# First passes of the down projection from the eleventh pair on, residual kept in DRAM meanwhile

## The chip, the cores and the metric
The kernel runs on one core of a Trainium2 chip. The metric is the device time of one execution in microseconds (us); lower is better. Engines in the profile: PE (matmuls) and PEld (weight loads into it), DVE (vector), ACT (activation), POOL, and SP, which here issues nearly all transfers (DMA). Each engine works through its instructions in a fixed order.

## The reference
One layer of an encoder on 256 tokens of width 2048, in float32: a mixer (latent attention and a two-way state-space scan, gated and added), then a gated MLP with a short convolution, then a final norm. The change lies in the MLP:

```
h = h + m @ W_out
h = h + conv_ffn(rms_norm(h, norm_ffn_w), ...)
out = rms_norm(h, norm_final_w)

def conv_ffn(h, w_up, conv_w, conv_b, w_down):
    u = centred_dwconv(h @ w_up, conv_w, conv_b)      # kernel of 3 over the tokens
    gate, val = jnp.split(u, 2, axis=-1)              # 5632 columns each
    return (jax.nn.silu(gate) * val) @ w_down         # 5632 -> 2048
```

## The kernel before
Channels lie on the 128 partitions, tokens run along a row. A float32 product is made of three products of rounded parts: each operand is split into a high part (made by ACT, line 220 or 150) and a low part (the difference, made by DVE, line 221 or 151). Weights are loaded from DRAM in slabs of 128 columns and 16 blocks of 128 rows (1 MB), into three buffers (`raw`), and split in halves of 8 blocks (`wh`, `wl`) into five pairs of buffers. L247 is the product of the high weights with both parts of the activations, L254 that of the low weights.

The MLP's first half, the up projection, has 44 pairs of slabs, a gate slab and a value slab each, numbered m = 0 to 43. The two slabs of a pair run as mates: both high products (32 matmuls of L247), then both low ones (32 of L254). The result goes through the convolution (L296, L297, L1093, L1095), the gate and a split to `aHL`, on ACT and DVE; two pairs make one tile of `aHL` (4 KB per partition) and one of sums, `aS`.

The norm before the up projection is done in two ways. For m under 9 (`TURNED`) the activations `hHL` are not scaled yet, and `conv3` multiplies by `r_ffn` (L1092). Meanwhile `rescale(j)`, j = 0 to 7, makes the scaled blocks (`nF`, L1082, L1083, L151) from the residual `h`, one in each of the pairs 1 to 8; from pair 9 on they are used.

The down projection's first 8 of 16 output blocks use a scheme of seven products on 2 x 2 blocks. Its first pass for two pairs of slabs, one tile kp of 22, is a unit (`unit_one`, 12 matmuls of L1142): it needs one weight load of 1 MB, sums of weights on DVE (L185, L186, L188, L189, tiles `T13`, `T24`) and their split (L150, L151). Units are put between pairs of the up projection, by the table `first` (pair m to kp). After a unit, part of `aS` goes to DRAM (`n4D`), and for kp under K0 also `aHL` (`aD`), so that its place is free.

After the up projection come the plain output blocks 8 to 15 (`down`: `d8`, ... for the second part of the rows, `a8`/`b8`, ... for the first part, L1243 adds into `h`), mixed with the second passes (`second`: `s20`, ...) and at the end the first 8 blocks (`seven_channels`, L1218). The list `seq` gives the order; `a_load` (L1208) and `n4_load` (L1204) bring back what was stored.

Tiles of 4 KB per partition come from one pool of 29 (`page`). The residual is in four of them, `hp[0]` to `hp[3]`, from the output projection to the end. A scheduler of the framework sets the order on each engine from the order in which the code emits, the dependences and its own estimates.

Of the kernel before, what the change touches and what calls it, by code (L numbers as in the profile page):

```python
# [8 lines left out]
F32 = mybir.dt.float32  # L9
# [6 lines left out]
P = 128  # L16
S = 256
# [47 lines left out]
def tile_bidir_hybrid_layer(ctx: ExitStack, tc, xT, pos, vec, cst, w_in, w_r, w_v, w_qk, w_oa,  # L65
                            w_os, w_out, w_up, w_dn, out, RAWB=3, HB=5, NPG=29, NP1=18):
    nc = tc.nc
# [5 lines left out]
    dr = ctx.enter_context(tc.tile_pool(name="dr", bufs=1, space=bass.MemoryType.DRAM))  # L73
# [3 lines left out]
    def page(shape, dt=F32, name="pg"):  # L77
        return pp.tile(shape, dt, tag="pg", bufs=NPG, name=name)
# [10 lines left out]
    def f32(ap):  # L89
        return ap.bitcast(F32)  # L90
# [17 lines left out]
    def vcol(name, i=0):  # L108
        o = VOFF[name] + i
        return V[:, o:o + 1]  # L110
# [38 lines left out]
    def hilo(wh, wl, v):  # L149
        act.activation(wh, v, AF.Copy)  # L150
        dve.tensor_sub(wl, v, f32(wh))  # L151
# [887 lines left out]
    hp, hHL = {}, {}  # L1039
# [37 lines left out]
    def rescale(j):  # L1077
        v = page([P, 2, S], name="nF")
        t = nF[j] = page([P, 2, 2, S], F32R, name="hHL")
        for b in range(2):  # L1080
            m = 2 * j + b
            act.activation(v[:, b, :], hp[m // 4][:, m % 4, :], AF.Identity, scale=vcol("nffn", m))  # L1082
        dve.tensor_mul(v, v, r_ffn["r"].unsqueeze(1).broadcast_to([P, 2, S]))  # L1083
        hilo(t[:, 0], t[:, 1], v)

    gv, aHL = {}, {}

# [212 lines left out]
    def at(slot, fn, *a):  # L1300
        late.append((slot, lambda: fn(*a)))
# [156 lines left out]
        at(b + max(4 * q, 0), x_load, q)  # L1458
    b = len(jobs)
    turns = [b]  # L1460
    K0, KE = 12, 14
    first = {7 + (36 * kp + 10) // 20: kp for kp in range(21)}
    assert len(first) == 21 and all(2 * kp + 2 <= m < NFF for m, kp in first.items())
    slots = []
    for m in range(NFF):
# [5 lines left out]
    for j in range(8):  # L1471
        at(slots[1 + j] + j % 2, rescale, j)
# [3 lines left out]
    lo, rest_of = {}, {}  # L1476
# [16 lines left out]
    turns.append(lo["d8"])  # L1493
    for g, w in enumerate("s20 b10 b11 d8 d10 s16".split()):
        at(lo[w], n4_load, g, min(4, NK - 4 * g))
    for kp in range(K0):
        at(lo["u21"] + (4 * kp) // 5 if kp < 10 else lo["a8"] + kp - 10, a_load, kp)
    for i in range(4):
        at(lo["a13"] + 1 + i, seven_channels, i)
    jobs[b].post.append(ffn_r)  # L1500
# [86 lines left out]
    while i < len(jobs):  # L1587
        j = jobs[i]
        first = base[i]
# [109 lines left out]
```

## Time and profile before
| | us |
|---|---|
| three runs | 1934.26, 1937.96, 1938.18; median 1937.96 |
| profiled execution | 1937.51 |
| its span (first to last instruction) | 1935.7 |
| output projection, last part, and up projection | about 1106 to 1762 of the span |
| down projection | about 1751 to 1925 |

A time of the profile is counted from the span's start. An engine's row gives start, length, engine, line, the tile written and those read, and how many such instructions are merged; a bracket gives the idle time before it and what ended it. DVE rows of before and after differ in line numbers by 8 (L1095 is L1103 after).

### The profile page before, as it was taken

To read this page: it belongs to the slowest core of one execution; us is meant where nothing else is said; L and a number is where in the kernel's file an instruction comes from. 1 tells how busy PE (TensorE), PEld (TensorE's weight loads), DVE (VectorE), ACT (ScalarE), POOL (GpSimd) and SP (SyncE) were. 2 spreads that over 40 slices of the span, in tenths; PEclk is the share of its full clock that TensorE was granted. 3 is DMA by queue.
4 is the path that set the end of the run, shared out by engine and by line. 5 is a ranking of instruction groups with operands and counts; after the bars stand their busy time and mean duration, and the time that the engine had idled before them with its cause. 6 is when DMAs were issued, how large, how long until landed. Compare 5 with 4: busy or idle time off the path is not lost.

```text
span 1935.7 us, 28865 instructions
## 1 busy us (share of the span) xinstructions
PE 1919.9 (99%) x10800; PEld 1677.9 (87%) x10800; DVE 1616.4 (84%) x2645; ACT 1286.4 (66%) x2049; POOL 16.2 (1%) x36
## 2 busy tenths in 40 slices
PE   9999999999999999999999999999999999999997
PEld 8899988888888888888888888888888888888887
DVE  7888778979779779779898886889889888888676
ACT  6565555878887888878665555765666666565554
POOL 0200000000000000000000000000000000000000
PEclk9999999999999999999999999999999999999999
DMA  7644547765665665565566675657666666668994
GB/s 284 206 156 150 164 132 228 273 220 174 215 230 168 212 239 169 202 239 169 173 195 201 216 250 176 214 199 245 243 235 233 223 223 217 212 238 306 315 292 143
DMA packets 171291, 415.20 MB, mean 214 GB/s; under 512 B 10640, under 2 KB 113744, under 8 KB 144272
## 3 DMA queue, kind: packets, MB, share of 16 engines
q1 hardware_dynamic: 169360, 410.74, 62.5%
q0 software_dynamic: 1024, 1.54, 0.3%
q8 instruction: 84, 1.38, 0.3%
q10 hardware_dynamic: 768, 1.09, 0.2%
q14 instruction: 55, 0.45, 0.1%
HBM read 398.56 MB, written 13.60 MB: 213 GB/s over the span
## 4 chain that ended last, share of the span: by engine, by line
PE 93%; DVE 3%; DMA 2%; ACT 1%; issue 0%; SPq 0%; DVEq 0%; ACTq 0%
PE g L247 37%; PE g L254 19%; PE g L965 11%; PE s L1142 5%; PE g L282 3%; PE g L283 3%; PE g L284 3%; PE s L965 2%; DMA raw<-in_w_dn 1%; PE g L226 1%; PE g L228 1%; PE g L227 1%; DVE wl L221 1%; PE s L247 1%; PE s L870 1%; PE s L879 1%
## 5 line engine op out<-in xcount | busy, mean ns | idle before, releaser
L221 DVE TENSOR_TENSOR wl<-raw,wh 128x1024 fp32r<-128x1024 f32 x590 | 708.6, 1214 | 173.9 <-ACT wh L220 95.3
L220 ACT ACTIVATE wh<-raw 128x1024 fp32r<-128x1024 f32 x590 | 609.4, 1048 | 254.3 <-PE g L247 82.2
L247 PE MATMUL g<-xHL,wh 128*128 128x512 f32 x1424 | 341.7, 392 | 0.2 <-DVE cu L297 0.2
L247 PE MATMUL g<-hHL,wh 128*128 128x512 f32 x1408 | 328.2, 390 | 0.0
L247 PEld LDWEIGHTS g<-hHL,wh 128*128 128x128 f32 x1408 | 263.4, 188 | 53.8
L247 PEld LDWEIGHTS g<-xHL,wh 128*128 128x128 f32 x1424 | 262.5, 188 | 52.1 <-PE s L228 0.4
L254 PEld LDWEIGHTS g<-xHL,wl 128*128 128x128 f32 x1424 | 182.6, 191 | 6.9
L254 PE MATMUL g<-xHL,wl 128*128 128x256 f32 x1424 | 184.7, 283 | 0.0
L254 PEld LDWEIGHTS g<-hHL,wl 128*128 128x128 f32 x1408 | 174.8, 192 | 3.4
L254 PE MATMUL g<-hHL,wl 128*128 128x256 f32 x1408 | 176.0, 283 | 0.0
L965 PE MATMUL g<-wh,yHL 128*128 128x512 f32 x392 | 124.9, 390 | 0.0
L150 ACT ACTIVATE wh<-raw 128x1024 fp32r<-128x1024 f32 (+1 forms) x108 | 80.5, 776 | 52.0 <-PE g L965 13.1
L151 DVE TENSOR_TENSOR wl<-raw,wh 128x1024 fp32r<-128x1024 f32 (+1 forms) x108 | 91.0, 876 | 23.1 <-ACT wh L150 15.1
L150 ACT ACTIVATE wh<-T 128x1024 fp32r<-128x1024 f32 x60 | 63.6, 1061 | 56.8 <-DVE T L189 21.4
L282 PE MATMUL g<-wh,xHL 128*128 128x512 f32 x256 | 100.4, 392 | 0.0
L283 PE MATMUL g<-wl,xHL 128*128 128x512 f32 x256 | 100.0, 391 | 0.0
L284 PE MATMUL g<-wh,xHL 128*128 128x512 f32 x256 | 99.8, 390 | 0.0
L1095 DVE SCALAR_TENSOR_TENSOR uc<-u,V,uc 128x255 f32<-128x255 f32 x176 | 84.6, 481 | 15.9 <-ACT uc L1093 14.8
L965 PEld LDWEIGHTS g<-wh,yHL 128*128 128x128 f32 x392 | 73.6, 188 | 15.2
L151 DVE TENSOR_TENSOR wl<-T,wh 128x1024 fp32r<-128x1024 f32 x60 | 73.4, 1223 | 15.8 <-ACT wh L150 13.2
L247 PE MATMUL g<-aHL,wh 128*128 128x512 f32 x338 | 79.8, 390 | 0.2 <-ACT wh L220 0.2
L1093 ACT ACTIVATE uc<-u,V 128x256 f32<-128x256 f32 x88 | 52.4, 595 | 40.9 <-DVE u L297 34.3
(389 smaller groups left out, 3120.0 us busy)
## 6 DMA issues: line engine op xcount, KB each, us to landing
raw<-in_w_in SPq DMA_DIRECT2D x88, 1024.0 KB, 4.9
raw<-in_w_up SPq DMA_DIRECT2D x88, 1024.0 KB, 4.8
raw<-in_w_in SPq DMA_DIRECT2D x128, 256.0 KB, 3.9
raw<-in_w_os SPq DMA_DIRECT2D x32, 1024.0 KB, 6.2
raw<-in_w_dn SPq DMA_DIRECT2D x30, 1024.0 KB, 5.1
raw<-in_w_oa SPq DMA_DIRECT2D x16, 1024.0 KB, 5.8
FB<-acsD SPq DMA_DIRECT2D x32, 512.0 KB, 7.3
raw<-in_w_dn SPq DMA_DIRECT2D x16, 896.0 KB, 5.1
```

The lines of the kernel that those rows point to most:

```text
L150: act.activation(wh, v, AF.Copy)
L151: dve.tensor_sub(wl, v, f32(wh))
L220: act.activation(vh, r, AF.Copy)
L221: dve.tensor_sub(vl, r, f32(vh))
L247: pe.matmul(ps, lhsT=wh[:, b, :], rhs=x, start=k == 0, stop=False)
L254: pe.matmul(cell["ps"][:, 0, :], lhsT=wl[:, b, :], rhs=get(k)[:, 0, :], start=False, stop=k == ktot - 1)
L282: pe.matmul(ps, lhsT=x[:, 0, ts], rhs=wH[:, kk, :], start=k == 0, stop=False)
L283: pe.matmul(ps, lhsT=x[:, 0, ts], rhs=wL[:, kk, :], start=False, stop=False)
L284: pe.matmul(ps, lhsT=x[:, 1, ts], rhs=wH[:, kk, :], start=False, stop=k == kt - 1)
L965: pe.matmul(M[nm], lhsT=x, rhs=w, start=left[nm] == total[nm], stop=left[nm] == 1)
L1095: dve.scalar_tensor_tensor(o[:, a], u[:, b], vcol("fcw", k * 88 + cb), o[:, a], ALU.mult, ALU.add)
L1142: pe.matmul(M[nm], lhsT=x, rhs=w, start=left[nm] == 3 * NK, stop=left[nm] == 1)
```

## The change
- `first`: the first unit comes after pair 10 instead of pair 7, and the 21 units of the up projection lie 33/20 pairs apart instead of 36/20. After pairs 10, 12, 13, 15, 17, 18, 20, ... 43 instead of 7, 9, 11, 12, 14, 16, ... 43.
- Each block of the residual is written to DRAM (`hD`) once two rescalings have read it, and its page is given up; four reads (`h_load`) bring it back: blocks 2 and 3 at `d8` and `d10`, blocks 0 and 1 at `a12` and `b12`.
- K0 is 10 instead of 12: ten tiles of `aHL` go to DRAM and back instead of twelve.

```
     def rescale(j):
...
+        if j % 2:
+            nc.sync.dma_start(hD[j // 2], hp.pop(j // 2))
+
+    hD = dr.tile([4, P, 4, S], F32, name="hD")
+
+    def h_load(q):
+        hp[q] = page([P, 4, S], name="h")
+        nc.sync.dma_start(hp[q], hD[q])
...
-    K0, KE = 12, 14
-    first = {7 + (36 * kp + 10) // 20: kp for kp in range(21)}
+    K0, KE = 10, 14
+    first = {10 + (33 * kp + 10) // 20: kp for kp in range(21)}
...
+    for q, w in ((2, "d8"), (3, "d10"), (0, "a12"), (1, "b12")):
+        at(lo[w], h_load, q)
     for kp in range(K0):
-        at(lo["u21"] + (4 * kp) // 5 if kp < 10 else lo["a8"] + kp - 10, a_load, kp)
+        at(lo["u21"] + (4 * kp) // 5 if kp < 8 else lo["a8"] + kp - 8, a_load, kp)
```

DVE's order behind the last weight half of pair 7 (`wl<-raw_12663` before, `wl<-raw_12666` after). `raw_12708` before is the first unit's weights; `raw_12712` and `raw_12788` after are the slabs of pair 8. Before:

```order
L221 TENSOR_TENSOR wl_12685<-raw_12663,wh_12684 128x1024
L151 TENSOR_TENSOR hHL_12666<-nF_12665,hHL_12666 128x512
L297 TENSOR_TENSOR u_12696<-u_12696,g_12617 128x256
L1092 TENSOR_TENSOR u_12696<-u_12696,r_ffn_11954 128x256
L1095 SCALAR_TENSOR_TENSOR uc_12697<-u_12696,V_72,uc_12697 128x255 x2
L1108 TENSOR_TENSOR uc_12697<-uc_12697,uc_12655 128x256
L1113 TENSOR_TENSOR aHL_12705<-uc_12697,aHL_12705 128x256
L1083 TENSOR_TENSOR nF_12710<-nF_12710,r_ffn_11954 128x512
L297 TENSOR_TENSOR u_12781<-u_12781,g_12727 128x256
L185 TENSOR_TENSOR T13_12719<-raw_12708 128x512
L151 TENSOR_TENSOR hHL_12711<-nF_12710,hHL_12711 128x512
L186 TENSOR_TENSOR T13_12719<-raw_12708 128x512
```

After, the same place:

```order
L221 TENSOR_TENSOR wl_12689<-raw_12666,wh_12688 128x1024
L151 TENSOR_TENSOR hHL_12669<-nF_12668,hHL_12669 128x512
L297 TENSOR_TENSOR u_12700<-u_12700,g_12620 128x256
L221 TENSOR_TENSOR wl_12722<-raw_12712,wh_12721 128x1024
L1100 TENSOR_TENSOR u_12700<-u_12700,r_ffn_11955 128x256
L1103 SCALAR_TENSOR_TENSOR uc_12701<-u_12700,V_72,uc_12701 128x255 x2
L221 TENSOR_TENSOR wl_12768<-raw_12712,wh_12767 128x1024
L1116 TENSOR_TENSOR uc_12701<-uc_12701,uc_12658 128x256
L297 TENSOR_TENSOR u_12779<-u_12779,g_12725 128x256
L221 TENSOR_TENSOR wl_12791<-raw_12788,wh_12790 128x1024
L1121 TENSOR_TENSOR aHL_12709<-uc_12701,aHL_12709 128x256
L1083 TENSOR_TENSOR nF_12714<-nF_12714,r_ffn_11955 128x512
```

The unit's sums (L185, L186) are gone from here, and the weight halves of pair 8 stand in between; the rescaling (L1083, L151) keeps its place among the convolution's rows.

DVE's order at the last first-pass unit, `u21`, between `d8`/`d9` and `d10` (`h_11272` and `h_17397` are block 2 of the residual, `g` the sums of `d8` and `d9`). Before:

```order
L189 TENSOR_TENSOR T24_17397<-T24_17397,raw_17390 128x512
L151 TENSOR_TENSOR wl_17395<-T13_17396,wh_17394 128x1024
L151 TENSOR_TENSOR wl_17447<-T24_17397,wh_17446 128x1024
L1243 TENSOR_TENSOR h_11272<-h_11272,g_17404 128x256
L221 TENSOR_TENSOR wl_17463<-raw_17460,wh_17462 128x1024
L1243 TENSOR_TENSOR h_11272<-h_11272,g_17404 128x256
```

After:

```order
L189 TENSOR_TENSOR T24_17402<-T24_17402,raw_17393 128x512
L151 TENSOR_TENSOR wl_17400<-T13_17401,wh_17399 128x1024
L1251 TENSOR_TENSOR h_17397<-h_17397,g_17409 128x256
L151 TENSOR_TENSOR wl_17452<-T24_17402,wh_17451 128x1024
L1251 TENSOR_TENSOR h_17397<-h_17397,g_17409 128x256
L221 TENSOR_TENSOR wl_17468<-raw_17465,wh_17467 128x1024
```

The first add into `h`, which now needs a read from DRAM, stands between the unit's two low halves. SP's order of transfers at the same place, before:

```order
L144 DMA raw_17488<-in_w_dn 128x2048
L1204 DMA n4_17392<-n4D_89 128x4x256
L1208 DMA aHL_17490<-aD_88 128x1024
L1208 DMA aHL_17492<-aD_88 128x1024
L1157 DMA n4D_89<-aS_17363 128x128 x2
```

and after:

```order
L144 DMA raw_17493<-in_w_dn 128x2048
L1212 DMA n4_17395<-n4D_90 128x4x256
L1092 DMA h_17397<-hD_88 128x1024
L1216 DMA aHL_17495<-aD_89 128x1024
L1216 DMA aHL_17497<-aD_89 128x1024
```

The read of block 2 takes the first reload's place, and the reloads of `aHL` come one place later.

## The prediction
> **What bounds the kernel now.** I read the page's head first, then busy time by stretches, then the PE's own rows where a stretch was short of work. The head:
> ```profile
> span 1935.7 us, 28865 instructions
> PE 1919.9 (99%) x10800; PEld 1677.9 (87%) x10800; DVE 1616.4 (84%) x2645; ACT 1286.4 (66%) x2049; POOL 16.2 (1%) x36
> ```
> PE is busy for 1919.9 of 1935.7 us, and the change takes no matmul away. What it can win is time in which PE waits or runs slow. The stretches (us, busy time of PE, PEld, DVE, ACT, POOL, clock, DMA share, GB/s) show where:
> ```profile
> 1153.00:1175.00 22.00, 22.00 (x128) 19.41 (x127) 15.12 (x25) 11.30 (x16) 0.00 (x0) 1.00 0.56 199
> 1242.00:1264.00 22.00, 22.00 (x128) 19.46 (x127) 20.59 (x38) 15.77 (x29) 0.00 (x0) 1.00 0.65 221
> 1344.00:1358.00 14.00, 14.00 (x78) 12.24 (x77) 12.85 (x23) 7.71 (x14) 0.00 (x0) 1.00 0.72 242
> 1787.00:1803.00 16.00, 16.00 (x88) 13.93 (x87) 10.64 (x17) 5.92 (x8) 0.00 (x0) 1.00 0.83 268
> 1838.00:1860.00 22.00, 21.76 (x110) 18.28 (x109) 16.61 (x20) 14.56 (x20) 0.00 (x0) 1.00 0.99 303
> ```
> (Pairs of slabs are numbered from 0, as in the code.) In these stretches PE is never idle, but for 0.24 us in the last. DVE is busy for 20.59 of 22 us in pairs 4 and 5, where rescaling is on, and for 12.85 of 14 in a pair that a down unit follows. So DVE is a close second, and at the end DMA is one, with 0.99 of the time. The one large gap is at the first down unit (start, length, group; in brackets the idle time before and what ended it):
> ```profile
> 1276.22 7.44 PE L247 MATMUL g<-hHL,wh 128*128 128x512 f32 x32
> 1283.50 3.99 PE L254 MATMUL g<-hHL,wl 128*128 128x256 f32 x32
> 1289.84 0.73 PE L1142 MATMUL s<-wh,aS 128*128 128x512 f32 x2 [2.35 <-ACT wh L150]
> 1291.42 0.79 PE L1142 MATMUL s<-wl,aS 128*128 128x512 f32 x1 [0.86 <-DVE wl L151]
> 1303.89 4.00 PE L254 MATMUL g<-hHL,wl 128*128 128x256 f32 x32
> ...
> 1339.95 4.00 PE L254 MATMUL g<-hHL,wl 128*128 128x256 f32 x32
> 1353.78 4.00 PE L254 MATMUL g<-hHL,wl 128*128 128x256 f32 x32
> ```
> An undisturbed run of L254, unit, L247 takes 1353.78 - 1339.95 = 13.83 us. Around the first unit it took 1303.89 - 1283.50 = 20.39. **The first unit costs 6.56 us more than a later one.** Part is idle time (2.35 and 0.86); the rest is the granted clock:
> ```profile
> 1288.00:1290.00 2.00, 0.16 (x1) 0.17 (x2) 2.00 (x5) 1.27 (x2) 0.00 (x0) 1.00 0.00 0
> 1291.00:1293.00 2.00, 1.58 (x4) 1.29 (x5) 2.00 (x4) 2.00 (x3) 0.00 (x0) 0.50 0.89 250
> 1295.00:1297.00 2.00, 2.00 (x6) 1.61 (x5) 2.00 (x5) 1.13 (x2) 0.00 (x0) 0.50 0.25 41
> ```
> PE does 0.16 us of work in 1288 to 1290 and afterwards gets a clock of 0.50. And why was the unit late? DVE's rows, and SP's issue of the unit's weights:
> ```profile
> 1279.83 1.22 DVE L221 TENSOR_TENSOR wl<-raw,wh 128x1024 fp32r<-128x1024 f32 x1
> ...
> 1283.11 1.00 DVE L1095 SCALAR_TENSOR_TENSOR uc<-u,V,uc 128x255 f32<-128x255 f32 x2 [0.67 <-ACT uc L1093]
> ...
> 1285.06 0.42 DVE L1113 TENSOR_TENSOR aHL<-uc,aHL 128x256 fp32r<-128x256 f32 x1 [0.48 <-ACT aHL L1112]
> 1285.86 0.69 DVE L1083 TENSOR_TENSOR nF<-nF,r_ffn 128x512 f32<-128x512 f32 x1 [0.38 <-ACT nF L1082]
> ...
> 1286.80 0.69 DVE L185 TENSOR_TENSOR T<-raw 128x512 f32<-128x512 f32 x1
> ...
> 1290.15 1.22 DVE L151 TENSOR_TENSOR wl<-T,wh 128x1024 fp32r<-128x1024 f32 x1
> 1268.85 0.38 SPq L138 DMA_DIRECT2D raw<-in_w_dn  x1
> ```
> The weights were asked for at 1268.85, 18 us ahead. DVE began on them (L185) at 1286.80, because its fixed order puts L185 behind the convolution of pair 6 and a rescaling step, and these waited on ACT three times (0.67, 0.48, 0.38). The unit's first low half began at 1290.15; PE had been free since 1287.5. The gap is one of DVE's order at the place where rescaling, the r_ffn multiplies and the first unit meet.
>
> **The change, part by part.** *The first unit moves from behind pair 7 to behind pair 10.* Rescaling ends with pair 8 and the r_ffn multiplies with pair 8, so the unit no longer stands among them. In the order of after the rows from there on hold four weight halves of pair 8 (L221), and L185 comes 48 rows further down. Gain: the 6.56 us. Whether it all goes depends on what is late next. That is the last rescaled block: pair 9 now follows without the pause, and its 15th matmul needs the block. By PE's rows it starts at 1276.22 + 2 x 11.12 + 14 x 0.2275 = 1301.65 (11.12 is a pair without unit: 7.28 and 3.84; 0.2275 is 7.28 / 32). DVE's starts one after another give the price of its rows:
> ```profile
> 1253.70 0.42 DVE L297 TENSOR_TENSOR u<-u,g 128x256 f32<-128x256 f32 x1
> 1254.03 0.69 DVE L1083 TENSOR_TENSOR nF<-nF,r_ffn 128x512 f32<-128x512 f32 x1
> 1254.63 0.42 DVE L1092 TENSOR_TENSOR u<-u,r_ffn 128x256 f32<-128x256 f32 x1
> 1254.97 1.22 DVE L221 TENSOR_TENSOR wl<-raw,wh 128x1024 fp32r<-128x1024 f32 x1
> 1256.11 0.48 DVE L1095 SCALAR_TENSOR_TENSOR uc<-u,V,uc 128x255 f32<-128x255 f32 x1
> 1256.50 0.69 DVE L151 TENSOR_TENSOR hHL<-nF,hHL 128x512 fp32r<-128x512 f32 x1
> ```
> From the row at 1279.83 to the end of that block, DVE has 37 instructions in the order of after: 8 weight halves at 1.14, 4 L151 at 0.60, 2 L1083 at 0.60, 7 convolution steps at 0.39, 4 L297 at 0.33, 4 r_ffn multiplies at 0.34, 4 products like them at 0.34, 4 sums of half the size at an estimated 0.25. That is 20.5 us, so 1300.3 without a wait. With the 1.53 us of waits on ACT that pair 7 shows it is 1301.9, with twice that 1303.4. PE would wait 0, 0.2 or 1.8 us. I take **0.3**, just over the middle case, which is the one that a row measures.
>
> A sentence of the Trainium skill bears on the price of the gap. "TensorE: Matmul & The Clock Gate", section "HAM oscillation — how this bites in real kernels", gives as its rule no PE-idle gaps above about 3.4 us. By that rule the 2.35 us gap would have left the clock alone, the old stall would be its 3.2 us of idle time, and the new time would come out near 1937.96 - 3.2 + 0.6 = 1935.4. The trace does not agree: the granted clock fell to 0.50 after it.
>
> *The other units come closer.* 21 units over 33 pairs leave seven one-pair intervals where there were four. PE's sum is the same. DVE has 14.00 - 12.85 = 1.15 us spare in such an interval, and no two come in a row; PE was busy for 14.00 of 14.00. Cost 0; if the cover went, PE would wait in L1142 for L151.
>
> *Residual to DRAM.* Four writes of 512 KB on SP's queue, which the order puts between weight loads of the output projection, one to every four slabs. Each waits at most for the last add into its block, which DVE does right behind the slab, while the next weight load waits for a buffer anyway. The DMA there is busy for 0.56 of the time at 199 GB/s (row 1153); 0.5 MB in four slabs (22 us) adds 24 GB/s. Cost 0; bounds 0 and one weight load late by the 2.6 us that 0.5 MB takes at that rate, which three buffers of 1 MB cover.
>
> The rows for the two parts that follow, in this order: the one late wait of PE; reloads on SP's queue; what two of them took to land (us at the end); DVE's and the chain's rows at the last first-pass unit.
> ```profile
> 1838.58 3.49 PE L247 MATMUL g<-aHL,wh 128*128 128x512 f32 x14 [0.24 <-ACT wh L220]
> ...
> 1754.49 1.18 SPq L1208 DMA_DIRECT2D aHL<-aD  x2
> ...
> 1787.09 0.50 SPq L1208 DMA_DIRECT2D aHL<-aD  x1
> 1789.11 0.43 SPq L1208 DMA_DIRECT2D aHL<-aD  x1
> ...
> aHL<-aD SPq DMA_DIRECT2D x2, 512.0 KB, 7.3
> aHL<-aD SPq DMA_DIRECT2D x1, 512.0 KB, 9.8
> ...
> 1759.41 2.50 DVE L151 TENSOR_TENSOR wl<-T,wh 128x1024 fp32r<-128x1024 f32 x2
> 1761.82 0.41 DVE L1243 TENSOR_TENSOR h<-h,g 128x256 f32<-128x256 f32 x1
> ...
> 1762.37 2.75 PE s L1142 x12
> ```
> *Two spills and two reloads fewer, four reads of h more.* Reads of h blocks 2 and 3 join the first burst, while the reloads at 1787.09 and 1789.11 go. The other two come in the stage from 1838 on: 1.05 MB, at 303 GB/s 3.5 us of a DMA that is busy for 0.99 there. But the two reloads that go give it as much room 50 us ahead, when the buffers can still run ahead. Bounds 0 and 3.5. PE's only wait there in before is 0.24 us; I take **0.3** lost net.
> *h block 2 gates DVE.* In the order of after the first add into h stands between the two low halves of the last first-pass unit (before: behind both). h is issued where the reload of 1754.49 was, so it lands 7.3 us later, at 1761.8. Then the add (0.33 to the next start) and the half (1.22) end at 1763.4. PE needs that half at 1762.37 + 1.37 + 0.23 = 1763.97. Spare 0.6; cost 0. With the longest landing of a reload here (9.8) PE would wait 1.9 us.
>
> **Sum.** -6.56 + 0.3 + 0.3 = -5.96 us. The profiled execution took 1937.51 (span 1935.7 and 1.8 around it), 0.45 under the median of 1937.96. So 1931.6 for the like of that execution and **1932.0** against the median. A difference of 0.2%, 3.9 us, is about what can be told from no change; the three runs themselves lie between 1934.26 and 1938.18, so a run in which the old stall costs less is possible.
>
> **The rivals.**
> *A new wait with a half clock* at h block 2: 1.9 us of waiting and the clock's share of the old stall, 6.56 - 3.2 = 3.4 (3.2 is 2.35 + 0.86). Then 1937.96 - 6.56 + 5.3 = 1936.7. For it: the 0.6 us of spare. Against: the same place in the queue landed in 7.3.
> *The late DMA takes it back.* Both late reads on the path: 1937.96 - 6.56 + 3.5 = 1934.9. For it: 0.99 busy. Against: the relief 50 us earlier.
> *Only the idle time comes back.* If the clock is halved as long at another place, 1937.96 - 3.2 + 0.6 = 1935.4. For it: the quickest run lies 3.7 us under the median, about the clock's share. Against: the half clock stands right behind the gap.
> *The stall moves with the unit.* If the order of DVE makes any first unit late, the gap comes behind pair 10 at the same price: 1938.0. Against: DVE has lost rescaling (L1083 and L151, 1.2 us a pair) and r_ffn (L1092, 0.7 a pair) two pairs before.
> *Slower: DVE becomes the bound in one-pair intervals.* Seven of them. If units there start as late as the first one did, each costs 6.56; the change loses from two such stalls on: 1937.96 - 6.56 + 2 x 6.56 = 1944.5. It decides where DVE brings more than its 1.15 us of arrears into the interval. Against: PE was busy for 14.00 of 14.00 us.
>
> **How the numbers follow.** Forecast 0.66, faster by more than 3.9 us while the two small terms stay under 2.6 together; 0.02 of it go to a comparison with a quicker before, as same. New wait 0.10, late DMA 0.08 and idle time alone 0.02, at 1934.9 to 1936.7: within 0.2%, but for 0.02 that are faster. Moved stall 0.08, of it 0.06 same and 0.02 slower. Dense units 0.06, slower. So faster 0.66, same 0.26, slower 0.08. The range goes from 1930.4 (the whole 6.56 and the 0.24, and 0.7 of scatter) to 1937.0, which takes in the two rivals that give part back.
>
> **What would show it.** Right: no idle time and a clock of 1.00 at the first unit, its two L151 done ahead of their matmuls; the span shorter by about 6 us, half of it idle time of PE and half matmuls at full clock. Pair 9 shows at most a short wait of L247 on DVE. Wrong: a clock of 0.50 anywhere after 1250; an add into h that waits for DMA beyond 1762.4; waits of L247 on ACT beyond 1840.

## The result, and the profile after

| | us |
|---|---|
| before, 10 runs beside those of after | median 1937.55 (1934.26 to 1938.28) |
| after, 10 runs | median 1932.19 (1930.61 to 1934.82) |
| ratio | 0.9977, 95% interval 0.9967 to 0.9987 |
| profiled execution of after | 1930.61, span 1928.8 |

The kernel became 5.4 us faster; the forecast was 1932.0, 6.0 us faster. The head of the page of after:

```profile
span 1928.8 us, 28860 instructions
PE 1915.7 (99%) x10800; PEld 1675.2 (87%) x10800; DVE 1615.0 (84%) x2645; ACT 1286.1 (67%) x2049; POOL 16.2 (1%) x36
```

Against before (span 1935.7, PE busy for 1919.9) the span is 6.9 us shorter: PE's busy time fell by 4.2 us with the same 10800 matmuls, and its idle time by 2.7 us (15.8 to 13.1). With the same work the busy time can only fall where matmuls run faster: 3.4 of the 4.2 us are the half clock that is gone (half of its 6.83 us); the other 0.8 was not traced. PE's rows of after from pair 8 to behind the first unit (start, length, group, in brackets the idle time before):

```profile
1294.14 4.00 PE L254 MATMUL g<-hHL,wl 128*128 128x256 f32 x32
1297.98 7.65 PE L247 MATMUL g<-hHL,wh 128*128 128x512 f32 x32
1305.46 4.00 PE L254 MATMUL g<-hHL,wl 128*128 128x256 f32 x32
1309.30 7.44 PE L247 MATMUL g<-hHL,wh 128*128 128x512 f32 x32
1316.58 4.00 PE L254 MATMUL g<-hHL,wl 128*128 128x256 f32 x32
1320.41 0.40 PE L1150 MATMUL s<-wh,aS 128*128 128x512 f32 x1
...
1322.05 0.50 PE L1150 MATMUL s<-wl,aS 128*128 128x512 f32 x1
...
1330.58 4.00 PE L254 MATMUL g<-hHL,wl 128*128 128x256 f32 x32
```

No bracket is left. From L254 to L254 across the first unit it is now 1330.58 - 1316.58 = 14.00 us, where before it took 20.39. Two small marks remain: pair 9's L247 takes 7.65 instead of 7.44, and one matmul of the unit 0.50 instead of 0.39. DVE's rows behind these two, and those at the last first-pass unit:

```profile
1300.45 0.68 DVE L151 TENSOR_TENSOR hHL<-nF,hHL 128x512 fp32r<-128x512 f32 x1
...
1317.82 1.23 DVE L151 TENSOR_TENSOR wl<-T,wh 128x1024 fp32r<-128x1024 f32 x1
...
1320.77 1.23 DVE L151 TENSOR_TENSOR wl<-T,wh 128x1024 fp32r<-128x1024 f32 x1 [0.80 <-ACT wh L150]
...
1754.69 0.42 DVE L1251 TENSOR_TENSOR h<-h,g 128x256 f32<-128x256 f32 x1 [0.72 <-DMA h<-hD]
1755.03 1.22 DVE L151 TENSOR_TENSOR wl<-T,wh 128x1024 fp32r<-128x1024 f32 x1
```

The last rescaled block is done at 1300.45 + 0.68 = 1301.13, and pair 9's 15th matmul wants it at 1297.98 + 14 x 0.2275 = 1301.17. By this it came just in time, yet the 15th matmul begins at 1301.28, 0.1 us late, and the one behind it loses as much again; that makes the 0.21 us. The first unit's low halves are ready at 1319.05 and 1322.00. The add into residual block 2 waited 0.72 us for its read; the half behind it still comes 0.9 us ahead of its matmul. The stretches of the first unit and of the late stage (us, busy time of PE, PEld, DVE, ACT, POOL, clock, DMA share, GB/s) are full, and the clock is 1.00. (At 1919.96, in the final norm, it falls to 0.50 until the end, as it did at 1928.92 before; the prediction's sign "a clock of 0.50 anywhere after 1250" did not leave out the end.) The two rows:

```profile
1316.00:1324.00 8.00, 8.00 (x51) 7.04 (x50) 7.21 (x12) 5.92 (x9) 0.00 (x0) 1.00 0.60 215
1832.00:1854.00 22.00, 22.00 (x117) 19.00 (x116) 16.72 (x21) 13.45 (x18) 0.00 (x0) 1.00 1.05 340
```

Following the same matmul through both traces, after is 0.4 us ahead when the first unit's place is reached (most of it from the kernel's first 15 us), 6.6 ahead behind it, 7.2 ahead from 1840 on, and 6.9 at the end. So pair 9 and the first unit gave 6.2 us, and the late stage 0.6 more.

### The profile page after: what moved, and what is told of

It reads as the page before. It is cut to its first block, busy times and chain, and to the rows that moved or that the text cites. A ratio compares the mean times of both kernels' runs of the same rounds, so it can differ in the third digit from the quotient of the medians.

```text
span 1928.8 us, 28860 instructions
## 1 busy us (share of the span) xinstructions
PE 1915.7 (99%) x10800; PEld 1675.2 (87%) x10800; DVE 1615.0 (84%) x2645; ACT 1286.1 (67%) x2049; POOL 16.2 (1%) x36
## 4 chain that ended last, share of the span: by engine, by line
PE 96%; DVE 1%; ACT 1%; DMA 1%; issue 0%; SPq 0%; DVEq 0%
PE g L247 38%; PE g L254 20%; PE g L965 11%; PE s L1150 5%; PE g L282 3%; PE g L283 3%; PE g L284 3%; PE s L965 2%; PE g L226 1%; PE g L228 1%; PE g L227 1%; PE s L247 1%; PE s L870 1%; PE s L879 1%; PE s L226 0%; PE s L227 0%
## 5 line engine op out<-in xcount | busy, mean ns | idle before, releaser
L247 PE MATMUL g<-xHL,wh 128*128 128x512 f32 x1424 | 341.7, 392 | 0.2 <-DVE cu L297 0.2
L247 PE MATMUL g<-hHL,wh 128*128 128x512 f32 x1408 | 327.4, 390 | 0.0
L247 PEld LDWEIGHTS g<-hHL,wh 128*128 128x128 f32 x1408 | 262.7, 188 | 53.7 <-ACT wh L220 0.3
L247 PEld LDWEIGHTS g<-xHL,wh 128*128 128x128 f32 x1424 | 262.5, 188 | 52.1 <-PE s L228 0.4
L254 PEld LDWEIGHTS g<-xHL,wl 128*128 128x128 f32 x1424 | 182.6, 191 | 6.9
L254 PE MATMUL g<-xHL,wl 128*128 128x256 f32 x1424 | 184.8, 283 | 0.0
L254 PEld LDWEIGHTS g<-hHL,wl 128*128 128x128 f32 x1408 | 174.8, 192 | 3.4
L254 PE MATMUL g<-hHL,wl 128*128 128x256 f32 x1408 | 176.0, 283 | 0.0
L151 DVE TENSOR_TENSOR wl<-raw,wh 128x1024 fp32r<-128x1024 f32 (+1 forms) x108 | 90.7, 873 | 19.2 <-ACT wh L150 12.6
L1103 DVE SCALAR_TENSOR_TENSOR uc<-u,V,uc 128x255 f32<-128x255 f32 x176 | 84.2, 478 | 14.3 <-ACT uc L1101 13.1
L151 DVE TENSOR_TENSOR wl<-T,wh 128x1024 fp32r<-128x1024 f32 x60 | 73.3, 1222 | 15.9 <-ACT wh L150 13.5
L247 PE MATMUL g<-aHL,wh 128*128 128x512 f32 x338 | 79.7, 390 | 0.0
L965 PE MATMUL g<-wl,yHL 128*128 128x512 f32 x196 | 76.3, 389 | 0.0
```

The lines of the kernel that those rows point to most:

```text
L247: pe.matmul(ps, lhsT=wh[:, b, :], rhs=x, start=k == 0, stop=False)
L254: pe.matmul(cell["ps"][:, 0, :], lhsT=wl[:, b, :], rhs=get(k)[:, 0, :], start=False, stop=k == ktot - 1)
L965: pe.matmul(M[nm], lhsT=x, rhs=w, start=left[nm] == total[nm], stop=left[nm] == 1)
L1103: dve.scalar_tensor_tensor(o[:, a], u[:, b], vcol("fcw", k * 88 + cb), o[:, a], ALU.mult, ALU.add)
```

## The experiments

What was open: whether the move or the pages bring the gain, whether the unit was late for the reason given, what the residual's transfers cost, and how a gap of 2.35 us could halve the clock. Each time is a median, with the range of its runs; the ratio is against runs of before on the same chip. Differences of about 1 us between kernels that were not timed side by side are not told apart.

**The change in two parts.** The DRAM part alone is the kernel after with

```
-    K0, KE = 10, 14
-    first = {10 + (33 * kp + 10) // 20: kp for kp in range(21)}
+    K0, KE = 12, 14
+    first = {7 + (36 * kp + 10) // 20: kp for kp in range(21)}
```

and `a_load` as before. Expected:

> The kernel after with its table of units put back (first unit behind pair 7, then 36/20 pairs apart) and twelve tiles of aHL spilled and reloaded as before: only the residual's way through DRAM (four writes, four reads, 4.2 MB) is left of the change. Theory (the gap is DVE's order at the first unit, the DRAM part costs nothing): the first unit is late again by about 2.4 us, the clock falls to 0.50 behind it, and the time is the one of before, 1937.5, within 1 us. Rival 1 (the first unit was late because places in the page pool were short, and the four freed pages cure that): about 1932. Rival 2 (the residual's transfers cost something late in the kernel, which the move hides in the kernel after): 1938.5 to 1941, with waits of PE beyond 1830.

Measured 1938.81 (1936.60 to 1940.46), ratio 1.0010 (1.0001 to 1.0019). PE's waits at the first unit, from the table of waits (us in total, times, longest):

```profile
PE s L1150 <- ACT wh L150: 2.3, 1, 2.3
PE s L1150 <- DVE wl L151: 0.7, 1, 0.7
```

PE's rows with a wait in the late stage:

```profile
1821.03 3.48 PE L247 MATMUL g<-aHL,wh 128*128 128x512 f32 x14 [0.18 <-ACT wh L220]
1839.84 3.49 PE L247 MATMUL g<-aHL,wh 128*128 128x512 f32 x14 [0.60 <-ACT wh L220]
1858.39 3.47 PE L247 MATMUL g<-aHL,wh 128*128 128x512 f32 x14 [0.33 <-ACT wh L220]
```

The first unit is late by 2.3 and 0.7 us as in before, so free pages do not cure it. Besides, PE now waits three times in the late stage, 1.11 us in sum, where before had 0.24. The theory's first half holds, and rival 2 holds in kind: the residual's way through DRAM costs something late, 1.1 us by these waits and 1.5 in the medians (1937.34 for before on the same chip).

The move alone is the kernel before with the new `first` and nothing else:

> The kernel before with the new table of units alone (first unit behind pair 10, then 33/20 pairs apart); the residual stays in its four pages, twelve tiles are spilled. Theory (the move brings the whole gain, the rest of the change costs and brings nothing, and is there for the pages): if the pool has a page whenever one is asked for, 1932, as after. The pool of 29 pages then has to hold, at pairs 8 to 10, 16 pages of scaled and unscaled activations, 4 of the residual, about 5 of aHL and 5 of sums, which leaves next to nothing: a late page makes DVE or ACT wait around pairs 8 to 11, and each PE gap of over 2 us there costs 5 to 7 us, so that 1935 to 1945 would show that the residual's way through DRAM is what pays for the move. Rival (the pages are a matter of the late stage only): no gap before 1320, but waits of reloads beyond 1750.

Measured 1931.55 (1930.61 to 1932.28), ratio 0.9973 (0.9962 to 0.9983). The whole gain comes from one line. The shortage of pages that I had worked out did not show: the first unit had one wait of 0.22 us for L151, and apart from it PE did not wait again until the last norm. The residual's way through DRAM and the spill count are not needed for the move.

**Why the first unit was late.** The last two rescalings are left out of the kernel before:

```
-    for j in range(8):
+    for j in range(6):
         at(slots[1 + j] + j % 2, rescale, j)
```

> The kernel before without the last two of the eight rescalings (the blocks for them stay unscaled, so this part of the computation is left out); the first unit stays behind pair 7. It tests why the unit was late. Theory as in the prediction (the rescaling rows L1083 and L151, with the wait on ACT for nF, stand ahead of the unit's rows on DVE): two rows of 0.60 us and a wait of 0.38 go from ahead of the first low half, and one row of L1095 of 0.39 moves behind it, so the halves come about 2 us earlier: 0.5 us ahead instead of 1.30 and 1.46 late. No gap over 0.3 us at the first unit, a clock of 1.00, a time of 1931 to 1932.5. Rival (DVE is in arrears from the r_ffn multiplies, or waits for ACT's convolution rows in any case): a gap of 1 us or more remains and the time is 1934 or more.

Measured 1932.46 (1931.44 to 1932.96), ratio 0.9971 (0.9960 to 0.9982). PE at the first unit:

```profile
1287.34 0.65 PE L1142 MATMUL s<-wh,aS 128*128 128x512 f32 x2
1288.80 0.50 PE L1142 MATMUL s<-wh,aS 128*128 128x512 f32 x1 [0.81 <-ACT wh L150]
```

The gap shrinks from 3.21 us (2.35 and 0.86) to 0.81, and nothing is left of the half clock. So the rescaling rows made 2.4 of the 3.2 us. They were not the whole: a gap of 0.81 stayed, where I expected none over 0.3. I had counted the low halves' lateness from the unit's own late start; counted from the moment PE was free, the first half was not 1.30 but 3.80 us late in before: the unit's second matmul could have begun at 1283.50 + 3.84 + 0.23 = 1287.57, and the half was done at 1291.37. Here it is 1.22 late.

Next, the first unit at other places in the kernel after, with `first = {8 + (35 * kp + 10) // 20 ...}`, `9 + (34 ...`, `11 + (32 ...`:

> The kernel after with the first unit behind pair 8 (then 35/20 pairs apart), the pair of the last rescaling. With the first unit behind pairs 7, 9, 10 and 11 its first low half came -1.30, -0.13, 1.60 and 3.19 us ahead of its matmul. Theory 1 (only rescaling rows ahead of the unit make it late; the last of them stands in this pair): late by about as much as behind pair 7, a gap of 1.5 to 2.5 us, 1933.5 to 1938. Theory 2 (DVE works off an arrear steadily, some 0.6 us or more a pair): late by 0.5 to 1 us, a gap too short for a half clock, 1933 to 1934.

> The kernel after with the first unit behind pair 9 (then 34/20 pairs apart), so one pair behind the last rescaling (pair 8) and the last multiply by r_ffn. Theory 1, as in the prediction (the old gap comes from the unit's rows standing among the rescaling and r_ffn rows): no gap, a time within 1 us of the one of after (1932.2). Theory 2 (DVE is in arrears as a whole after the rescaling pairs and needs two pairs to catch up; in the kernel after the first unit's two low halves came only 1.60 and 0.01 us ahead, the later ones 1.9 to 3.2 and 0.9 to 3.0): the unit behind pair 9 comes 1 to 2 us late, which gives a gap of PE of that length near 1309, a half clock behind it if it is long enough, and 1933.5 to 1938.

> The kernel after with the first unit behind pair 11 (then 32/20 pairs apart: eight one-pair intervals). Both theories on the old gap: no gap at the first unit, its low halves more than 2 and 0.8 us ahead (after: 1.60 and 0.01). If the scatter of the kernel after (1930.6 to 1934.8 in ten runs) comes from the second low half that was only 0.01 us ahead, the runs come closer together and the median falls to about 1931; if not, the median stays at 1932 with the same scatter. If the denser units or the later start use up the pages or DVE's 1.15 us of spare time, single gaps appear in the one-pair intervals: 1934 to 1938.

| first unit behind pair | 7 (before) | 8 | 9 | 10 (after) | 11 |
|---|---|---|---|---|---|
| first low half, us ahead of the unit's second matmul, had PE not waited | -3.80 | -0.77 | -0.13 | 1.60 | 3.19 |
| PE's gaps there, us | 3.21 | 1.14 | none shown | none shown (0.18 in a second profile) | none |
| median of the runs | 1937.55 | 1934.01 | 1932.30 | 1932.19 | 1931.41 |
| range of the runs | 1934.26 to 1938.28 | 1932.54 to 1936.36 | 1931.07 to 1933.85 | 1930.61 to 1934.82 | 1930.79 to 1933.94 |
| ratio, 95% interval | | 0.9984 (0.9975 to 0.9994) | 0.9976 (0.9967 to 0.9984) | 0.9977 (0.9967 to 0.9987) | 0.9973 (0.9964 to 0.9983) |

Behind pairs 7, 8 and 9 the order on PE puts the low half's first matmul third, 0.23 us later, so that -0.13 gives no wait. The three gaps behind pair 8, with the clock at 1.00 throughout:

```profile
1301.36 0.50 PE L1150 MATMUL s<-wl,aS 128*128 128x512 f32 x1 [0.43 <-DVE wl L151]
...
1303.05 0.50 PE L1150 MATMUL s<-wh,aS 128*128 128x512 f32 x1 [0.50 <-ACT wh L150]
...
1304.00 0.73 PE L247 MATMUL g<-hHL,wh 128*128 128x512 f32 x2 [0.21 <-ACT wh L220]
```

Behind pair 8, which holds the last rescaling, the unit is late by 1.14 us in sum; behind pair 9, one pair past the last rescaling, it still has nothing to spare (though 0.13 us, not the 1 to 2 that theory 2 gave, so the time is as theory 1 has it); 3.19 ahead is reached behind pair 11. Only rescaling rows in the way (theory 1) would give a step after pair 8, and the values climb over four pairs. So DVE is in arrears after the rescaling and works them off from pair to pair, as theory 2 has it in kind, and the place of the rows adds to that behind pair 7. The trace of the run with the first unit behind pair 11 shows the arrear itself, undisturbed by a unit: the last DVE row of the convolution (`aHL`, L1121) ends 8.7 to 12.1 us behind the matmuls of its pair in pairs 2 to 8, 6.6 behind in pair 9 and 4.9 in pair 10, as in later pairs that no unit follows. The eight one-pair intervals of the unit behind pair 11 show no gap either.

**What the late transfers cost.** After once more, and after with twelve tiles spilled (`K0, KE = 12, 14`), side by side:

> The kernel after, unchanged, so that the others of this group are compared with it on the same chip, and for a second profile of it. Expected: 1932.2 within 0.7. If its scatter (1930.6 to 1934.8) comes from the late stage, where DMA is busy for 0.95 to 1.05 of the time, the second profile has waits of L247 on ACT (L220) beyond 1815 of up to 1 us in sum, as the run that only brought the residual's transfers had (0.18, 0.60 and 0.33); if it comes from the first unit, whose second low half was 0.01 us ahead, a wait of L1150 near 1321.

> The kernel after with twelve tiles of aHL spilled and reloaded, as before, instead of ten: 1 MB more to write and 1 MB more to read. It sizes the late DMA. Theory (the late stage is at the edge of what DMA brings; the two reloads that the change drops pay for the residual's four reads): waits of L247 on ACT beyond 1815 of about 1.1 us in sum, as with the residual's transfers alone, and 1933.0 to 1933.6. Rival (the transfers are hidden either way): 1932.2 and no waits. The prediction's upper bound for this term was 3.5 us.

After came to 1932.79 (1931.36 to 1934.28), with twelve tiles to 1934.49 (1932.27 to 1936.65); ratios 0.9975 (0.9964 to 0.9985) and 0.9984 (0.9975 to 0.9993). Two more tiles each way cost 1.7 us in the medians, more than the 0.8 to 1.4 expected. The profiled execution of the second was its fastest and shows one late wait of 0.18 us only, so where the 1.7 us arise is not shown. The second profile of after does show late waiting:

```profile
1833.28 3.49 PE L247 MATMUL g<-aHL,wh 128*128 128x512 f32 x14 [0.88 <-ACT wh L220]
```

That wait of 0.88 us was absent from the first profile of after. The same program waits here in one execution and not in the next. The spans of the two profiles differ by 2.0 us, and following the same matmul through both, 1.2 of it arise in the late stage, 0.3 at pair 9 and the first unit, and 0.4 ahead of the MLP. So the late stage is the largest part of what these two differ by; the wider scatter of the other runs has no profile. Of the nine profiles here with the residual's way through DRAM, six show late waits of L247 (0.18 to 1.11 us in sum) and three none; of the four with the residual in its pages, two show one (0.24 and 0.22) and two none.

The read of residual block 2, three reloads later (run late_h2):

```
+    for kp in range(3):
+        at(lo["d8"], a_load, kp)
     for q, w in ((2, "d8"), (3, "d10"), (0, "a12"), (1, "b12")):
         at(lo[w], h_load, q)
-    for kp in range(K0):
+    for kp in range(3, K0):
```

> The kernel after with three reloads of aHL (1.5 MB) issued ahead of the read of residual block 2 instead of behind it. It tests the prediction's reading that this block gates DVE, and through it the second low half of the last first-pass unit. In the kernel after the block landed at 1754.63 and the half was done 0.9 us ahead of its matmul. Theory: the block lands 4 to 5 us later (1.5 MB at 300 to 400 GB/s), DVE stands before the half, PE waits 3 to 4 us near 1757, the clock falls to 0.50 behind it, and the time is 1935 to 1939. Rival (the add is not in the way, or the queues share the bandwidth so that the block lands no later): 1932.

Measured 1937.61 (1935.90 to 1939.03), ratio 0.9999 (0.9990 to 1.0008): all of the gain is lost. DVE's rows and PE's at the unit:

```profile
1760.99 0.42 DVE L1251 TENSOR_TENSOR h<-h,g 128x256 f32<-128x256 f32 x1 [5.57 <-DMA h<-hD]
1761.32 1.22 DVE L151 TENSOR_TENSOR wl<-T,wh 128x1024 fp32r<-128x1024 f32 x1
...
1762.60 0.50 PE L1150 MATMUL s<-wl,aS 128*128 128x512 f32 x1 [3.15 <-DVE wl L151]
```

And stretches of busy time around it (columns as above):

```profile
1757.34:1760.75 3.41, 2.11 (x10) 1.39 (x8) 0.00 (x0) 2.48 (x3) 0.00 (x0) 1.00 1.03 404
1760.75:1764.16 3.41, 1.56 (x7) 1.30 (x8) 3.17 (x5) 0.80 (x2) 0.00 (x0) 1.00 0.34 144
1764.16:1767.58 3.42, 3.42 (x17) 2.81 (x16) 3.42 (x5) 1.82 (x2) 0.00 (x0) 1.00 0.44 101
```

DVE stands for 5.57 us before the add and the half, until the block is there, and the half comes 3.15 us late: the gate is real, and 0.9 us of spare was all that hid it. Against the expectation, the clock of this execution stayed at 1.00 behind a gap of 3.15 us.

**Which gaps halve the clock.** In all 13 traces here the lengths between two changes of the clock are whole multiples of 3.413 us (but for the last, which the end cuts): in before the half clock lasted 6.827 (2 of them) and the full clock after it 631.466 (185). The grid of these lengths lies 0.3 to 3.3 us behind the first matmul, by the trace (0.6 and 3.1 in the two traces of after), so the kernel does not set it. So the clock is judged at fixed times, and what counts should be the idle time between two of them. The rows of late_h2 above are two such stretches: PE was busy for 2.11 and 1.56 us, idle for 1.30 and 1.85, and nothing changed. The same view of before (each row but for rounding one such stretch):

```profile
1287.21:1290.63 3.42, 1.01 (x5) 0.37 (x3) 3.42 (x7) 1.91 (x5) 0.00 (x0) 1.00 0.00 0
1290.63:1294.04 3.41, 2.62 (x6) 2.13 (x7) 3.41 (x5) 3.40 (x5) 0.00 (x0) 0.50 0.84 281
1294.04:1297.45 3.41, 3.41 (x9) 2.64 (x9) 3.41 (x6) 2.54 (x3) 0.00 (x0) 0.50 0.30 79
1297.45:1300.86 3.41, 3.41 (x16) 2.78 (x16) 1.88 (x4) 2.07 (x4) 0.00 (x0) 1.00 0.86 324
```

Idle for 2.41 us of the first: half a clock in the next two. To test it, gaps were made on purpose in the kernel after, by doing one of DVE's sums several times over at eight units:

```
+    EXTRA = {1: 6, 3: 8, 6: 8, 9: 9, 12: 8, 14: 9, 17: 10, 20: 8}
...
+            for _ in range(EXTRA.get(getattr(jobs[i], "kp", None), 0)):
+                dve.tensor_add(t[:, 1], B22, B12)
             dve.tensor_add(t[:, 1], B22, B12)
```

> The kernel after with gaps made on purpose: at eight of the units one of DVE's sums is done 6 to 10 times over (0.60 us each) ahead of the unit's split, at the units behind pairs 12, 15, 20, 25, 30, 33, 38 and 43, so that PE should stand still for about 1 to 4 us at each. It asks which gaps halve the clock. In the traces so far the clock changed only at multiples of 3.413 us, counted backwards from its last change, and a gap of 3.15 us left it alone in one run (its idle time lay in two such stretches, 1.31 and 1.84 us of them) while one of 2.35 us halved it (2.35 to 2.41 us of idle time in one stretch). Theory 1 (idle time within one fixed stretch of 3.413 us decides, with the bound between 1.84 and 2.35 us): each gap can be foretold from where its idle time lies. Theory 2 (the length of the gap decides, above about 3.4 us): only gaps over 3.4 us halve it. Theory 3 (what decides is not PE's idle time): no order in it.

Measured 1988.79 (two runs, 1988.50 and 1989.08). PE's rows behind the shortest gap (a second one of 0.22 us follows it) and behind one of the longer:

```profile
1349.89 0.73 PE L1154 MATMUL s<-wh,aS 128*128 128x512 f32 x2 [3.04 <-ACT wh L150]
...
1465.52 1.22 PE L1154 MATMUL s<-wh,aS 128*128 128x512 f32 x2 [5.12 <-ACT wh L150]
```

The stretches around these two:

```profile
1344.38:1347.79 3.41, 2.47 (x21) 2.27 (x19) 3.34 (x8) 1.37 (x3) 0.00 (x0) 1.00 0.00 0
1347.79:1351.21 3.42, 1.10 (x4) 0.63 (x5) 2.63 (x5) 2.85 (x4) 0.00 (x0) 1.00 0.32 96
1351.21:1354.62 3.41, 3.41 (x10) 2.67 (x9) 3.41 (x4) 3.41 (x5) 0.00 (x0) 0.50 0.61 212
1354.62:1358.03 3.41, 3.41 (x16) 2.79 (x15) 3.41 (x6) 0.55 (x2) 0.00 (x0) 1.00 0.76 250
1460.43:1463.85 3.42, 0.00 (x0) 0.00 (x0) 3.35 (x8) 1.40 (x3) 0.00 (x0) 1.00 0.00 0
1463.85:1467.26 3.41, 1.70 (x3) 0.98 (x4) 3.11 (x5) 2.85 (x3) 0.00 (x0) 0.50 0.55 161
1467.26:1470.67 3.41, 3.41 (x9) 2.64 (x9) 3.41 (x5) 3.25 (x5) 0.00 (x0) 0.50 0.35 147
1470.67:1474.09 3.42, 3.42 (x16) 2.78 (x16) 3.40 (x4) 2.13 (x2) 0.00 (x0) 1.00 0.89 287
```

The gaps came out longer than meant (3.0 to 7.1 us), and all eight halved the clock. All of this fits theory 1: each fall stands at the end of a stretch with 2.32 us or more idle (68%). Theory 2 fails: 3.04 us halved the clock here and 3.15 did not in late_h2. The half clock lasts one stretch where that one is full of work (row 1351.21, then 1.00) or nearly (0.22 us idle) and two or more where it is not (row 1463.85: busy for 1.70, and half a clock again in the one behind). The largest idle time in a stretch without a fall, in the middle of a kernel, was 1.85 us, the smallest with one 2.32; between the two nothing was measured. One thing does not fit: in the last 20 us of a kernel, where the matmuls are of another kind, the clock fell after stretches with 1.4 to 1.9 us idle as well. What the chip counts as work there stays open.

The Trainium skill, "TensorE: Matmul & The Clock Gate", section "Part 1: The HAM clock gate (the "warmup" mystery)", states a window of 3413 ns that runs freely, without regard to the kernel's start. The lengths here agree with it to the nanosecond, and so does the place of the grid, which differs from trace to trace. Its rule in the section "HAM oscillation — how this bites in real kernels", no PE-idle gaps above about 3.4 us, is not enough here: 2.35 us halved the clock.

So the same gap should halve the clock in one execution and not in the next, by where it falls. Both profiles with the old gap (before, and the DRAM part alone) have the half clock; that others have less of it is read from the mean granted clock of each run. In the 68 runs of before that stood beside the experiments:

| mean clock | runs | median us |
|---|---|---|
| 0.998 | 7 | 1934.66 |
| 0.997 | 26 | 1936.73 |
| 0.995 or 0.996 | 35 | 1938.03 |

One stretch at half clock is 3.41 / 1935 / 2 = 0.0009 of the mean, so the rows are no stretch, about one, and two. From the first to the last it is 3.4 us, half of 6.83. The classes are not clean: of 62 runs of the seven kernels that have no such gap, 15 also show 0.997 (none less), and in the one of these that was profiled (the unit behind pair 11) the half clock at the kernel's end took 10.5 us of the span, against 6.8 to 9.1 in the other profiles. The ten runs of late_h2 fall apart alike (0.998 once at 1935.90, 0.996 five times, median 1938.48).

**Without the DRAM part, later still.** The kernel before with `first = {11 + (32 * kp + 10) // 20 ...}`, K0 = 10 and `a_load` as after:

> The kernel before with the first unit behind pair 11 (32/20 pairs apart) and ten tiles spilled instead of twelve; the residual stays in its pages. Drawn from two runs: with the move alone the time was 1931.55, and with the first unit behind pair 11 its low halves were 3.19 and 2.98 us ahead. Theory (the residual's way through DRAM only costs, by late DMA; the move alone gains): no gap at the first unit, no wait of PE beyond 1820, and 1930.9 to 1931.5, 0.5 to 1 us under the kernel after, with runs closer together. Rival (the pages given up by the residual are needed once ten instead of twelve tiles are spilled): waits of ACT or DVE for a page in the last pairs, PE gaps beyond 1700, and 1933 to 1940.

Measured 1931.53 (1931.13 to 1931.96), ratio 0.9969 (0.9956 to 0.9981), beside 1932.79 (1931.36 to 1934.28) for after on the same chip. Its profile shows no wait of PE from 1240 on until the end of the late stage. It is the kernel I would keep: it needs less code and its runs lie closest together. That it is faster than after is likely, with five runs against eight, but not settled.

## Why the prediction was right, point by point

- *The stall of 6.56 us.* It went, in the profile to within 0.4 us (0.21 stay in pair 9, 0.17 in the unit). But 6.56 is what one execution lost. Idle time was 3.2 and 3.0 us in the two profiles that have the gap, and the half clock adds 0, 1.7 or 3.4 by chance: with the 68 runs above (7, 26 and 35) that is 2.4 in the mean, so 5.6 in all (an estimate that takes the middle class for one stretch). The term was set by the one profiled execution where the mean over executions was wanted, so it was about 1 us too large. With 5.6 in its place, 0.4 for pair 9 and the unit, and the late stage as the two profiles of after have it against before (0.6 gained, 0.7 lost), the sum is -5.8 to -4.5; the medians give -5.4, and -4.9 when after was run again. That the time came within 0.2 us of the forecast is partly luck: the difference was missed by 0.6, and before came out 0.4 lower than in the forecast.
- *Why the unit was late.* The rescaling rows were right for 2.4 of 3.2 us. The rest fits the arrear of DVE, which the convolution's rows show until pair 9 and the unit's lead until pair 11, and which the prediction touched only where it argued against the moved stall.
- *Pair 9, 0.3.* 0.21 (7.65 - 7.44), and the block was done at 1301.13, only just when it was needed, where the price list gave 1300.3 to 1301.9. Not forecast: the first unit's second half has 0.01 us to spare, and costs 0.1 to 0.2.
- *The late DMA, 0.3.* Probably too small, though within its bounds of 0 and 3.5. The profile of after shows no wait there, and even the 0.24 of before is gone; the second profile shows 0.88, and the DRAM part alone 1.11. The step that failed was to net the four reads against the two reloads from one execution, in a stage where the wait comes and goes. Two tiles each way were worth 1.7 us in the medians (the ranges overlap), and the residual's way through DRAM cost 1.5, so the third part of the change about pays for the second.
- *Block 2 of the residual.* Landing 6.8 us after its issue (forecast 7.3, from the neighbouring reloads), spare 0.9 (0.6), cost 0. That it would gate DVE was shown by delaying it.
- *Closer units, and the writes.* Cost 0, both right: no gap in seven intervals, nor in eight; with the DRAM part alone the lag against before does not grow between the writes and 1820.
- *The clock.* The prediction set the trace's 2.35 us against the rule of 3.4 and was right for this gap, and the clock's share came back with the idle time, as forecast. Its reading that such a gap halves the clock was too simple: it depends on how the gap lies to the fixed stretches. The quick run of 1934.26, which the prediction set beside the rival that only the idle time comes back, lies near the median of the runs with the highest mean clock (1934.66), so most likely it had the old gap without the half clock.

## What to carry to other kernels

Where the matrix engine is bound by the engine that feeds it, add up that engine's arrears over several steps, not only the rows that stand ahead of the late one: here the last rescaling is in pair 8, the convolution's rows had caught up by pair 10 and the unit's lead was full by pair 11. A single profile shows one throw of a die when a gap is near the length that halves the clock; the mean clock of all runs tells how often it falls, and a gap that can't be removed is best cut to under 1.8 us of idle time in any 3.4 us. Before a change that makes room is combined with the move it is meant for, run the move alone: here it needed no room.

## What the runs showed of the hardware that was not expected

The granted clock is judged every 3.413 us at times that the kernel does not set (the grid lies 0.3 to 3.3 us behind the first matmul, by the trace). In the middle of a kernel, 2.32 us or more of idle time within one such stretch halved it in all ten cases, up to 1.85 us in none; it came back after one stretch with at most 0.22 us idle, and stayed at half over a stretch in which PE was idle for 0.69 us or more. In the last 20 us, 1.4 us was enough once, and why is open. A gap of 3.15 us that was split 1.30 and 1.85 over two stretches cost nothing but itself.
